# One encoder layer on one core: the first FFN's opening stage fetches its modulation and its first token half ahead, with the operand sums on VectorE

## The chip, the core and the metric

The kernel runs on one core of a Trainium2 chip. The metric is the time of one execution in device microseconds (us), median of several runs; lower is better. The engines go by the names of the profile: PE is TensorE (matmuls; PEld its weight loads), DVE is VectorE, ACT is ScalarE, POOL is GpSimd, SP is SyncE. SP and ACT also issue the DMA transfers of this stage.

## What is computed

One layer of a bidirectional encoder on 1024 tokens of width 1024, in float32: a half-step SwiGLU FFN, a mixer of a convolution group and a differential-attention group, and a second half-step FFN, each with a residual and a LayerNorm behind it. Shift, scale and gate of each sub-layer come from one conditioning vector. The change touches only the beginning of the first FFN:

```python
c_act = jax.nn.silu(c)
mod = (c_act @ w_ada[l] + b_ada[l]).reshape(B, N_SUBLAYERS, 3, D)   # D = 1024, w_ada is 1024 x 9216

def swiglu(h, w_in, w_out):                                         # d_ff = 2816
    gate, up = jnp.split(h @ w_in, 2, axis=-1)
    return (jax.nn.silu(gate) * up) @ w_out

def post_norm_sublayer(x, mod, weight, f, g, b):
    shift, scale, gate = mod[:, 0, None, :], mod[:, 1, None, :], mod[:, 2, None, :]
    y = f(x * (1.0 + scale) + shift)
    return layer_norm(ALPHA * x + weight * (1.0 + gate) * y, g, b)
```

## The kernel before

**Products.** A float32 product is made of three matmuls: each operand is split into a rounded high part (a cast on ACT, `S.copy`) and the rest (a subtraction, on DVE unless told otherwise), and high by high, high by low and low by high are added in PSUM. `split` does this; its two lines show in the profile as L139 and L140. The input product of the FFN runs over 22 tiles `j` of 128 gate and 128 up columns. In each tile the two token halves and the gate/up pair form a 2 x 2 block product, which is done with seven products (A11·B11, A12·B21, S2·T2, S1·T1, S3·T3, S4·B22, A22·T4) over sums and differences of the operands. A product has 4 inner steps of 3 matmuls, each of 128x512; so a tile is 84 such matmuls. Their names in the rows are `fi_<tile>A` and `fi_<tile>S`. The left operands come from the weights (`ra`, `rb` as loaded; `ah`, `al`, `sh`, `sl` as split), the right ones from the modulated tokens and are kept for all 22 tiles: per pair `kk` of 128-row feature blocks (4 pairs) `r_kbh`/`bl` (first token half), `r_kt1h`/`t1l` and `r_kt3h`/`t3l` (differences of the halves) and `r_kb` (the second half's odd block).

**The opening stage.** For each pair `kk`, `first_ada` fetches 2 x 1024 x 256 values of `w_ada` (2 MiB) and `first_x` 1024 tokens x 256 features (1 MiB). `first_mod` makes shift and scale as two columns each, `B0` and `A0`: for some columns DVE adds the eight weighted rows (`ada0a`) and PE sums over partitions with `ones`; for the rest PE multiplies with `c_act` directly. PE transposes the tokens (`hT`), ACT or DVE applies scale and shift (`h`), POOL and DVE form the differences (`right_second`, `right_third`), and the splits follow.

**What sets the order.** Each engine runs its own queue in order; the queues are written by the program and a scheduler. In the opening stage the string `SEQ` gives the order: `a`/`x` fetch a pair, `M13` makes the modulation of pair 1 with 3 of its 4 column blocks on DVE, `H` transposes and modulates both token halves, `R` makes all right operands of the pair with an engine letter for each step, `g` runs four of tile 0's seven products for the pair. So each pair goes through everything before the next. All transfers are issued by SP. Buffers named by `slot` are 30 rotating slots of the tag `h`; the modulation weights of three of the pairs lie in part in the six buffers `sh`/`sl` instead. After the stage, tile 1 is prepared and `in_phase` runs the tiles one after the other: products 1, 2, 6, 5, 7, 3, 4 of tile 0, then those of tile 1, and so on.

Of the kernel before, what the change touches and what calls it, by code (L numbers as in the profile page):

```python
# [44 lines left out]
SEQ = "a0 M03 w0 x0 G0 a1 H0d x1 R0VGVGV M12 x2 a2 H1 M24 S0 g0 a3 R1VGVGG H2 g1 x3 R2VGVGG M33 H3d R3VVVGV g2 g3"  # L46
# [4 lines left out]
def layer_kernel(ctx, tc, a, out):  # L51
# [37 lines left out]
    S.activation(c_act, c_raw, AF.Silu)  # L89
# [190 lines left out]
    def right_first(name, ops, hb, eng=V):  # L280

        hi, lo = slot(f"{name}bh"), slot(f"{name}bl")
        split(hi, lo, hb, eng)
        ops["B11"].append((hi[:, 0], lo[:, 0]))
        ops["B21"].append((hi[:, 1], lo[:, 1]))

# [45 lines left out]
    def in_load(wp, s, w_in, j):  # L332
# [6 lines left out]
        for dst, src in ((ra[:, 0], k1[:, :, g]), (ra[:, 1], k2[:, :, g]), (rb, k1[:, :, u]), (ra[:, 2], k2[:, :, u])):  # L339
            SY.dma_start(dst, src)  # L340
# [353 lines left out]
    with pool("p1a") as wp:  # L694
        in_tags(wp, "ra rb ah al sf sh sl")
        ops = new_ops()
# [3 lines left out]
        def first_ada(kk):  # L700
            raws = []
            for m in range(2):
                for q in range(2):
                    name = f"ada0_{kk}_{m}{q}"
                    if kk == 0 or kk == 3 and m == 1:
                        raw = slot(name, (P, 4, 256), F32)
                    else:
                        raw = wp.tile([P, 4, 256], F32, tag="sl" if q else "sh", bufs=3, name=name)
                    SY.dma_start(raw, w_ada[:, 4 * q : 4 * q + 4, m * D + kk * 256 : m * D + (kk + 1) * 256])
                    raws.append(raw)  # L710
            return raws

        def first_x(kk):
            cols = slice(kk * 256, (kk + 1) * 256)
            xc = []
            for half in range(2):
                x = slot(f"xc{kk}_{half}", (P, 4, 256), F32)
                SY.dma_start(x, x_in[half * H : (half + 1) * H, cols].rearrange("(t p) n -> p t n", p=P))
                xc.append(x)
            return xc  # L720

        def first_mod(kk, raws, n):

            ps = wide(f"ada0p{kk}")
            if n:
                acc = wp.tile([P, 2, 256], F32, tag="ada_acc", bufs=1, name=f"ada0a{kk}")
            parts = [(m, max(0, 4 - n - 2 * m) * P) for m in (0, 1)]
            for j in range(KD):
                for m, lo in parts:
                    if lo >= 256:  # L730
                        continue
                    raw, dst = raws[2 * m + j // 4][:, j % 4, lo:], acc[:, m, lo:]
                    if j == 0:
                        V.tensor_scalar(dst, raw, c_act[:, 0:1], None, ALU.mult)
                    else:
                        V.scalar_tensor_tensor(dst, raw, c_act[:, j : j + 1], dst, ALU.mult, ALU.add)
            for m, lo in parts:
                for e in range(2):
                    es = slice(e * P, (e + 1) * P)
                    o = ps[:, 2 * m + e : 2 * m + e + 1]  # L740
                    if e * P >= lo:
                        PE.matmul(o, lhsT=acc[:, m, es], rhs=ones[:, 0:1], start=True, stop=True)
                        continue
                    for j in range(KD):
                        PE.matmul(
                            o, lhsT=raws[2 * m + j // 4][:, j % 4, es], rhs=c_act[:, j : j + 1],
                            start=j == 0, stop=j == KD - 1,
                        )
# [4 lines left out]
        def first_t(kk, xc, half):  # L753
            ps = wide(f"hT0_{kk}_{half}")
            for e in range(2):
                for i in range(4):
                    o = e * H + i * P
                    PE.transpose(ps[:, o : o + P], xc[half][:, i, e * P : (e + 1) * P], ident)
            return ps

        def first_h(kk, ps, half, HD):
            h = slot(f"h0_{kk}_{half}", dt=F32)
            k = 2 * kk
            h_of(h[:, 0], ps[:, 0:H], A0, B0, k)
            if HD:
                V.tensor_scalar(h[:, 1], ps[:, H:T], A0[:, k + 1 : k + 2], B0[:, k + 1 : k + 2], ALU.mult, ALU.add)
            else:
                h_of(h[:, 1], ps[:, H:T], A0, B0, k + 1)
            return h

        def early(wp, s, w_in, ops):
            order = (("A11", "B11"), ("A12", "B21"), ("S2", "T2"), ("S1", "T1"))
            begun = {}
            ada, xs_, hs, w, L0 = {}, {}, {}, [], {}

            def go(k):
                for left, right in order:
                    if left not in begun:
                        begun[left] = bank(f"fi{s}_0{left}")
                    product(begun[left], L0[left], ops[right], (k,))  # L780

            for tok in SEQ.split():
                c, k, v = tok[0], int(tok[1]), tok[2:]
                if c == "a":
                    ada[k] = first_ada(k)
                elif c == "x":
                    xs_[k] = first_x(k)
                elif c == "w":  # L790
                    w.append(in_load(wp, s, w_in, 0))
                elif c == "G":
                    L0.update(in_gate(wp, s, 0, w[0]))
                elif c == "S":
                    in_sums(wp, s, 0, w[0], L0, G if v else V)
                elif c == "M":
                    first_mod(k, ada[k], int(v))
                elif c == "H":
                    for half in range(2):
                        hs[k, half] = first_h(k, first_t(k, xs_[k], half), half, v == "d")  # L800
                elif c == "R":
                    e = [{"V": V, "G": G}[n] for n in v]
                    right_first(f"r0_{k}", ops, hs[k, 0], e[0])
                    t12 = right_second(f"r0_{k}", ops, hs[k, 0], hs[k, 1], e[1], e[2])
                    last = right_third(f"r0_{k}", ops, hs[k, 0], hs[k, 1], t12, e[3], e[4])
                elif c == "g":
                    go(k)
            raws = in_load(wp, s, w_in, 1)
            with tc.issue_after(last[0]), tc.issue_after(last[1]):
                L1 = in_gate(wp, s, 1, raws)  # L810
                in_sums(wp, s, 1, raws, L1)
            return [L0, L1], (begun, {}), None

# [673 lines left out]
```

## Time and profile before

| | us |
|---|---|
| median of 3 runs (1926.94 to 1928.09) | 1926.99 |
| profiled execution | 1927.3 |
| its span in the trace | 1925.5 |
| outside the span (start and end) | 1.8 |
| PE busy in the span | 1829.6 (95%) |
| DVE busy | 1518.1 (79%) |
| ACT busy | 773.0 (40%) |
| POOL busy | 321.0 (17%) |

The page's row of slices shows PE busy 5 and 8 tenths in the first two of 40 slices (48 us each), and nine tenths or more in nearly all others. An engine's busy time includes matmuls that overlap. The granted clock of PE is 0.974 of full in the mean.

### The profile page before, as it was taken

The numbers are of one execution on the slowest core, as the hardware profiler recorded it, in microseconds if no ns is written. First come the engines' busy times: TensorE is split into PE (matmuls) and PEld (weight loads), VectorE is DVE, ScalarE is ACT, GpSimd is POOL, SyncE is SP. The second block draws the span as 40 slices with busy tenths as digits, with TensorE's granted clock in tenths as the row PEclk, the third lists the DMA queues.
The fourth block names the chain that finished last, engine by engine and source line by source line (L and its number), as shares of the span: only waits on it lengthen the run. The fifth ranks groups of instructions, "written<-read, shape, count | busy, mean of one in ns | idle before, by whom it ended". The sixth has DMA issues, their size and how long they took to land.

```text
span 1925.5 us, 23435 instructions
## 1 busy us (share of the span) xinstructions
PE 1829.6 (95%) x8562; PEld 1512.7 (79%) x8562; DVE 1518.1 (79%) x2306; ACT 773.0 (40%) x1233; POOL 321.0 (17%) x236
## 2 busy tenths in 40 slices
PE   5899999999999999999999877989999999999996
PEld 4688888888888878888788765868887888888885
DVE  8867767765698887999688889898767565569789
ACT  3423333333445442142477761353333333254540
POOL 3200000000000010067376562160000000000000
PEclk7899999999999999999999888989999999999998
DMA  8526545442985332111000033125555333177432
GB/s 252 167 96 212 170 150 175 157 144 89 307 302 155 120 116 66 44 44 34 1 1 1 12 121 99 55 82 168 174 162 175 120 116 120 44 287 275 133 99 83
DMA packets 203699, 246.79 MB, mean 128 GB/s; under 512 B 14122, under 2 KB 124831, under 8 KB 203582
## 3 DMA queue, kind: packets, MB, share of 16 engines
q1 hardware_dynamic: 199082, 231.61, 37.0%
q0 software_dynamic: 2112, 7.34, 1.0%
q10 hardware_dynamic: 2388, 6.33, 0.8%
q8 instruction: 67, 1.10, 0.2%
q14 instruction: 50, 0.41, 0.1%
HBM read 188.08 MB, written 57.15 MB: 127 GB/s over the span
## 4 chain that ended last, share of the span: by engine, by line
PE 70%; DVE 16%; issue 8%; DMA 3%; ACT 2%; POOL 1%; SPq 1%; DVEq 0%; POOLq 0%; ACTq 0%
PE fo L589 19%; PE mo L1294 4%; PE vp L961 2%; DVE mx L1058 2%; PE qp L961 2%; PE fi_16A L378 1%; PE fi_15A L378 1%; PE fi_10A L378 1%; PE fi_6A L378 1%; PE fi_2A L378 1%; PE fi_21A L378 1%; PE fi_19A L378 1%; PE fi_20A L378 1%; PE fi_18A L378 1%; PE fi_17A L378 1%
## 5 line engine op out<-in xcount | busy, mean ns | idle before, releaser
L589 PE MATMUL fo<-wr,gl 128*128 128x512 f32 x1848 | 423.1, 390 | 0.2
L589 PEld LDWEIGHTS fo<-wr,gl 128*128 128x128 f32 x1848 | 345.9, 188 | 75.3 <-DVE pv L632 1.3
L140 DVE TENSOR_TENSOR sl<-sf,sh 128x1024 fp32r<-128x1024 f32 x87 | 109.4, 1259 | 116.0 <-ACT sh L139 115.8
L139 ACT CAST sh<-sf 128x1024 fp32r<-128x1024 f32 x88 | 92.7, 1053 | 207.3 <-issue 31.3
L932 DVE SCALAR_TENSOR_TENSOR cacc<-u,convw,cacc 128x1015 f32<-128x1015 f32 (+14 forms) x120 | 150.7, 1305 | 0.9
L399 POOL DMA_DIRECT2D gd<-gf x8 | 4.5, 567 | 826.6 <-DVE gf L465 826.0
L140 DVE TENSOR_TENSOR gl<-gr,gl 128x512 fp32r<-128x512 f32 x148 | 102.1, 696 | 6.9 <-ACT gl L139 5.5
L139 ACT CAST gl<-gr 128x512 fp32r<-128x512 f32 x148 | 90.5, 617 | 24.3 <-DMA gr<-gd 17.6
L153 DVE SCALAR_TENSOR_TENSOR ada<-adaw,c_act,ada 128x512 f32<-128x512 f32 x98 | 73.2, 747 | 30.9 <-DMA adaw<-in_w_ada_dram 30.0
L1058 DVE TENSOR_REDUCE mx<-sc 128x1 f32<-128x1024 f32 x64 | 76.2, 1215 | 20.4 <-PE sc L1056 20.4
L1060 ACT ACTIVATE p<-sc,mx 128x1024 f32<-128x1024 f32 x64 | 71.4, 1115 | 47.8 <-DVE mx L1058 46.3
L139 ACT CAST ah<-ra 128x1536 fp32r<-128x1536 f32 x44 | 65.0, 1478 | 59.6 <-DMA ra<-in_ffn_w_in_dram 14.9
L140 DVE TENSOR_TENSOR al<-ra,ah 128x1536 fp32r<-128x1536 f32 x44 | 77.0, 1750 | 1.3 <-ACT ah L139 1.2
L427 ACT ACTIVATE gf<-gf 128x512 f32<-128x512 f32 x44 | 27.8, 632 | 124.1 <-DVE gf L426 113.7
L139 ACT CAST wr<-wa 128x512 fp32r<-128x512 f32 x66 | 41.2, 624 | 76.6 <-PE fo L589 76.0
L1294 PE MATMUL mo<-moh,fh 128*128 128x512 f32 x128 | 51.4, 402 | 20.7 <-DVE x L1298 20.1
L140 DVE TENSOR_TENSOR wr<-wa,wr 128x512 fp32r<-128x512 f32 x66 | 45.5, 689 | 27.4 <-ACT wr L139 27.2
L139 ACT CAST wr<-wb 128x512 fp32r<-128x512 f32 x66 | 40.2, 621 | 64.8 <-PE fo L589 51.5
L913 PE MATMUL glu<-hm,gluh 128*128 128x512 f32 x256 | 65.7, 392 | 0.0
L1112 POOL TENSOR_TENSOR p<-p,p 128x1024 f32<-128x1024 f32 x27 | 64.8, 2400 | 1.9
L1129 PE MATMUL av<-vf,aT 128*128 128x128 f32 x512 | 63.4, 278 | 1.2 <-ACT cacc L1190 0.8
L1129 PEld LDWEIGHTS av<-vf,aT 128*128 128x128 f32 x512 | 60.9, 195 | 1.7 <-ACT cacc L1190 1.0
(3505 smaller groups left out, 4775.6 us busy)
## 6 DMA issues: line engine op xcount, KB each, us to landing
gr<-gd SPq DMA_DIRECT2D x148, 256.0 KB, 3.3
ra<-in_ffn_w_in_dram SPq DMA_DIRECT2D x132, 256.0 KB, 3.8
adaw<-in_w_ada_dram SPq DMA_DIRECT2D x56, 512.0 KB, 3.8
gd<-gf SPq DMA_DIRECT2D x102, 256.0 KB, 2.1
rb<-in_ffn_w_in_dram SPq DMA_DIRECT2D x44, 256.0 KB, 3.0
wb<-in_ffn_w_out_dram SPq DMA_DIRECT2D x44, 256.0 KB, 5.4
wa<-in_ffn_w_out_dram SPq DMA_DIRECT2D x44, 256.0 KB, 5.0
gd<-s SPq DMA_DIRECT2D x40, 256.0 KB, 2.0
```

The costliest lines, as they stand in the source:

```text
L139: a = S.copy(hi, x)
L140: b = eng.tensor_tensor(lo, x, hi.bitcast(F32), ALU.subtract)
L153: V.scalar_tensor_tensor(acc, raw[:, jj], c_act[:, n : n + 1], acc, ALU.mult, ALU.add)
L378: pe_last[:] = [PE.matmul(ps, lhsT=w[:, k], rhs=x, start=k == 0 and n == 0 and not more, stop=k == 3 and n == 2, skip_group_check=more,).ins]
L589: PE.matmul(ps, lhsT=g[:, x, ts_], rhs=w[:, y], start=n in (1, 2, 3) and k == i == 0, stop=k == NK - 1 and i == 2, skip_group_check=n not ...
L913: PE.matmul(q[2 * m + h], lhsT=w[:, m * P : (m + 1) * P], rhs=hm[k][h][:, x], start=k == 0 and n == 0, stop=k == KD - 1 and n == 2,)
L932: V.scalar_tensor_tensor(acc[:, lo_t:hi_t], u[:, lo_t + sh : hi_t + sh], convw[:, i, jj : jj + 1], acc[:, lo_t:hi_t], ALU.mult, ALU.add,)
L961: PE.matmul(pss[t], lhsT=hk[:, x, ts_], rhs=w, start=k == 0 and n == 0, stop=k == KD - 1 and n == 2)
L1058: V.tensor_reduce(mx_, ps, axis=AX.X, op=ALU.max, negate=True)
L1060: S.activation(pe, ps, AF.Exp, bias=mx_, accum_out=sm[:, e : e + 1])
L1129: PE.matmul(ps[:, 0:P], lhsT=aT[:, kt], rhs=vf[kt][:, h * P : (h + 1) * P], start=kt == 0, stop=kt == 7)
L1294: pe = PE.matmul(ps, lhsT=x[:, ts_], rhs=w[:, ds_], start=n == 0, stop=n == total - 1)
```

## The change

Four things change, all in the opening stage and in tiles 0 and 1.

- **Fetch.** Every pair's modulation weights go to rotating slots, as four slots of 512 KiB filled by two transfers each. SP first issues, pair by pair, modulation and the first token half (512 tokens), then tile 1's weights, then the second token half of all pairs. Tile 0's weights are issued by ACT behind the first activation.
- **Modulation.** DVE adds six of the eight rows for all four columns of a pair (128x512 each), PE multiplies the last two rows with `c_act` into the same sum.
- **Order.** The first token half of all pairs is done first (`early`): modulation, transpose, scale, split, products A11·B11 and A12·B21 of tile 0. Then `mid` runs A11·B11 and A12·B21 of tile 1, the second token half of the pairs one by one with S2·T2 and S1·T1, and the remaining products of tiles 0 and 1 in turns.
- **Engines.** The differences of the halves, which POOL made for the most part, are on DVE; POOL has no work in the stage. Scale and shift are always on ACT.

```diff
-SEQ = "a0 M03 w0 x0 G0 a1 H0d x1 R0VGVGV M12 x2 a2 H1 M24 S0 g0 a3 R1VGVGG H2 g1 x3 R2VGVGG M33 H3d R3VVVGV g2 g3"
...
-            ps = wide(f"ada0p{kk}")
...
+            ps = bank(f"ada0p{kk}")
+            acc = wp.tile([P, 2, 256], F32, tag="ada_acc", bufs=1, name=f"ada0a{kk}")
+            for j in range(2 * n):
+                raw = raws[j // 2][:, j % 2]
+                if j == 0:
+                    V.tensor_scalar(acc, raw, c_act[:, 0:1], None, ALU.mult)
+                else:
+                    last = V.scalar_tensor_tensor(acc, raw, c_act[:, j : j + 1], acc, ALU.mult, ALU.add)
+            for i in range(4):
+                m, es = i // 2, slice(i % 2 * P, (i % 2 + 1) * P)
+                o = ps[:, i : i + 1]
+                for j in range(2 * n, KD):
+                    PE.matmul(
+                        o, lhsT=raws[j // 2][:, j % 2, m, es], rhs=c_act[:, j : j + 1], start=j == 2 * n, stop=False
+                    )
+                pe = PE.matmul(o, lhsT=acc[:, m, es], rhs=ones[:, 0:1], start=n == 4, stop=True)
...
+            with tc.issue_after(c_silu.ins):
+                raws = [in_load(wp, s, w_in, 0, S)]
+            ada, xb = [], []
+            for kk in range(4):
+                ada.append(first_ada(kk))
+                xb.append(first_x(kk, 0))
+            raws.append(in_load(wp, s, w_in, 1))
+            xc = [first_x(kk, 1) for kk in range(4)]
+            hb, L = [], [{}, {}]
             begun = {}
...
+            for kk in range(4):
+                with tc.issue_after(columns) if kk else nullcontext():
+                    summed, columns = first_mod(kk, ada[kk], 3)
+                    hb.append(first_h(kk, xb[kk], 0))
...
+                copied, rest = right_first(f"r0_{kk}", ops, hb[kk])
+                for left, right in (("A11", "B11"), ("A12", "B21")):
+                    if kk == 0:
...
+        def mid(st):
...
+            for kk in range(4):
+                with tc.issue_after(first["pe"]):
+                    b, h = hb[kk], first_h(kk, first["xc"][kk], 1)
+                t = wp.tile([P, 2, H], F32, tag="t12", bufs=1, name="t12_0") if kk == 0 else slot(f"t12_{kk}", dt=F32)
+                V.tensor_tensor(t[:, 0], h[:, 0], b[:, 0], ALU.subtract)
+                V.tensor_tensor(t[:, 1], h[:, 1], t[:, 0], ALU.subtract)
+                copied, rest = right_t(f"r0_{kk}", ops, 1, t)
...
+            for kk in range(4):
+                b, h, t = hb[kk], hc[kk], t12[kk]
+                right_b22(f"r0_{kk}", ops, h)
+                V.tensor_tensor(h[:, 0], h[:, 1], h[:, 0], ALU.subtract)
+                V.tensor_tensor(h[:, 1], b[:, 1], t[:, 1], ALU.subtract)
+                copied, rest = right_t(f"r0_{kk}", ops, 3, h)
```

The order of instructions shows where the work stands now. **PE, between the modulation of pairs 1 and 2.** `ada0p` are the modulation columns, `fi_0A` tile 0's two products. Before:

```order
L745 MATMUL ada0p_293<-c_act,ada_1_01_238 128x1 x4
L378 MATMUL fi_0A_397<-r_0bh,ah_0_232 128x512
L758 MATMUL hT_1_0_335<-ident,xc_0_268 128x128 x7
L742 MATMUL ada0p_293<-ones,ada0a_294 128x1 x2
L758 MATMUL hT_1_0_335<-ident,xc_0_268 128x128
L378 MATMUL fi_0A_397<-r_0bl,ah_0_232 128x512
```

Now:

```order
L748 MATMUL hT_2_0_390<-ident,xc_0_230 128x128 x8
L380 MATMUL fi_0A_302<-r_1bh,ah_0_294 128x512
L380 MATMUL fi_0A_306<-r_1bh,ah_0_294 128x512
L380 MATMUL fi_0A_302<-r_1bl,ah_0_294 128x512
L380 MATMUL fi_0A_302<-r_1bh,al_0_295 128x512
L380 MATMUL fi_0A_306<-r_1bl,ah_0_294 128x512
L380 MATMUL fi_0A_306<-r_1bh,al_0_295 128x512
L737 MATMUL ada0p_368<-ones,ada0a_369 128x1
L734 MATMUL ada0p_368<-c_act,ada_2_3_227 128x1 x2
```

All six products of a pair, which need that pair's split `r_1bl`, now stand ahead of the next pair's modulation columns; before, a pair's columns were made between them.

**DVE, the same place.** `B` and `A` are shift and scale, `ada0a` the sum over rows. Before:

```order
L140 TENSOR_TENSOR r_0bl<-h_0_0_253,r_0bh 128x1024
L736 SCALAR_TENSOR_TENSOR ada0a_294<-ada_1_11_242,c_act,ada0a_294 128x256 x2
L140 TENSOR_TENSOR r_0t1l<-r_0t_276,r_0t1h 128x1024
L140 TENSOR_TENSOR r_0b_286<-h_0_1_265,r_0b_286 128x512
L750 TENSOR_TENSOR B_105<-ada0p_293,bada 128x2
L751 SCALAR_TENSOR_TENSOR A_104<-ada0p_293,bada 128x2
```

Now:

```order
L739 TENSOR_TENSOR B_106<-ada0p_324,bada 128x2
L740 SCALAR_TENSOR_TENSOR A_105<-ada0p_324,bada 128x2
L727 TENSOR_SCALAR ada0a_369<-ada_2_0_218,c_act 128x512
L729 SCALAR_TENSOR_TENSOR ada0a_369<-ada_2_0_218,c_act,ada0a_369 128x512
L729 SCALAR_TENSOR_TENSOR ada0a_369<-ada_2_1_221,c_act,ada0a_369 128x512 x2
L141 TENSOR_TENSOR r_1bl<-h_1_0_355,r_1bh 128x1024
L729 SCALAR_TENSOR_TENSOR ada0a_369<-ada_2_2_224,c_act,ada0a_369 128x512 x2
L739 TENSOR_TENSOR B_106<-ada0p_368,bada 128x2
L740 SCALAR_TENSOR_TENSOR A_105<-ada0p_368,bada 128x2
```

The splits of the second half are gone from between the pairs, and a pair's row sums start behind the previous pair's `A`.

**DVE, the second token half.** `t_2` are the differences of the halves of pair 2. POOL made them before (these are POOL's rows):

```order
L290 TENSOR_TENSOR r_2t_486<-h_2_1_463,h_2_0_451 128x512
L291 TENSOR_TENSOR r_2t_486<-h_2_1_463,r_2t_486 128x512
L297 TENSOR_TENSOR r_2t_493<-h_2_1_463 128x512
L298 TENSOR_TENSOR r_2t_493<-h_2_0_451,r_2t_486 128x512
L140 TENSOR_TENSOR r_2t3l<-r_2t_493,r_2t3h 128x1024
```

Now, on DVE:

```order
L807 TENSOR_TENSOR t_2_546<-h_2_1_543,h_2_0_399 128x512
L808 TENSOR_TENSOR t_2_546<-h_2_1_543,t_2_546 128x512
L827 TENSOR_TENSOR h_2_1_543<-h_2_1_543 128x512
L141 TENSOR_TENSOR r_2t1l<-t_2_546,r_2t1h 128x1024
L807 TENSOR_TENSOR t_3_565<-h_3_1_562,h_3_0_443 128x512
L808 TENSOR_TENSOR t_3_565<-h_3_1_562,t_3_565 128x512
```

Three of the five moved to DVE beside the first split; the other two (`L828` and the split `r_2t3l`) come in a second round over the pairs, when the first round is done.

## Rows read from the trace of the kernel before

**Rows 1.** Stretches: us, busy PE, PEld, DVE, ACT, POOL (x count), PEclk, DMA, GB/s

```profile
20.00:53.00 33.00, 22.87 (x90) 18.82 (x91) 31.56 (x49) 14.13 (x19) 14.24 (x10) 0.59 0.76 236
...
76.00:103.00 27.00, 27.00 (x119) 22.09 (x118) 25.64 (x36) 10.35 (x13) 0.00 (x0) 1.00 0.56 169
```

**Rows 2.** Chain that ended last, first 140 us: start us, us, what

```profile
33.62 5.81 DVE ada0a L736 x7
...
102.72 5.44 PE fi_2A L378 x24
```

**Rows 3.** SP's waits, first 80 us: total us, times, longest

```profile
SPq L709 <- DVE ada0a L736: 14.9, 2, 7.7
```

**Rows 4.** Stretches of 10 us, columns as in Rows 1

```profile
0.00:10.00 10.00, 4.22 (x19) 4.05 (x19) 4.28 (x14) 1.49 (x2) 0.70 (x6) 1.00 0.82 248
10.00:20.00 10.00, 5.36 (x30) 5.04 (x30) 8.14 (x16) 3.67 (x4) 0.56 (x1) 1.00 1.11 332
20.00:30.00 10.00, 7.35 (x38) 6.47 (x39) 8.74 (x12) 3.85 (x5) 4.67 (x4) 0.57 1.09 348
30.00:40.00 10.00, 5.83 (x21) 4.53 (x19) 9.93 (x17) 6.33 (x8) 5.16 (x4) 0.67 0.47 146
```

**Rows 5.** Instructions on the tile ada, whole span: ns min/median/max

```profile
L153 DVE SCALAR_TENSOR_TENSOR ada<-adaw,c_act,ada x98: 734/746/754, 93.3 to 1540.7; 128x512 f32<-128x512 f32 x98
...
L151 DVE TENSOR_SCALAR ada<-adaw,c_act x14: 471/479/487, 92.3 to 1530.5; 128x512 f32<-128x512 f32 x14
```

**Rows 6.** A group by form, first 103 us: busy us, mean ns

```profile
L736 DVE SCALAR_TENSOR_TENSOR ada0a<-ada,c_act,ada0a 128x256 f32<-128x256 f32 x35 | 23.3, 679 | 0.6
```

**Rows 7.** Timeline, first 60 us: start us, us, engine, instruction

```profile
18.94 4.75 PE L745 MATMUL ada0p<-c_act,ada 128*128 128x1 f32 x32 [0.40 <-DVE h L766]
...
21.25 0.96 DVE L734 TENSOR_SCALAR ada0a<-ada,c_act 128x256 f32<-128x256 f32 x1 [1.05 <-DMA ada<-in_w_ada_dram]
...
30.70 1.22 DVE L140 TENSOR_TENSOR r_0t3l<-r_0t,r_0t3h 128x1024 fp32r<-128x1024 f32 x1
31.11 0.63 PE L378 MATMUL fi_0A<-r_0bl,ah 128*128 128x512 f32 x1
...
31.54 0.63 PE L378 MATMUL fi_0A<-r_0bh,al 128*128 128x512 f32 x1
...
31.96 1.91 PE L758 MATMUL hT<-ident,xc 128*128 128x128 f32 x8
...
33.91 1.45 ACT L277 ACTIVATE h<-hT,B,A 128x512 f32<-128x512 f32 x2 [1.85 <-PE hT L758]
...
36.18 1.05 ACT L139 CAST r_1bh<-h 128x1024 fp32r<-128x1024 f32 x1
...
56.23 2.27 DVE L140 TENSOR_TENSOR r_2bl<-h,r_2bh 128x1024 fp32r<-128x1024 f32 x1
```

**Rows 8.** Timeline, 60 to 86 us, columns as in Rows 7

```profile
65.61 1.09 PE L378 MATMUL fi_0A<-r_3bh,ah 128*128 128x512 f32 x2 [3.42 <-ACT r_3bh L139]
...
75.14 1.75 DVE L140 TENSOR_TENSOR al<-ra,ah 128x1536 fp32r<-128x1536 f32 x1
...
77.41 0.68 DVE L357 TENSOR_TENSOR sf<-ra,rb 128x512 f32<-128x512 f32 x1
...
78.01 0.68 DVE L356 TENSOR_TENSOR sf<-sf,ra 128x512 f32<-128x512 f32 x1
...
81.28 0.39 PE L378 MATMUL fi_1A<-r_1bh,ah 128*128 128x512 f32 x1
...
81.51 0.39 PE L378 MATMUL fi_1A<-r_1bl,ah 128*128 128x512 f32 x1
```

**Rows 9.** Stretches of 1 us, PE alone: busy (x count), PEclk, DMA, GB/s

```profile
52.00:53.00 1.00, 1.00 (x5) 0.93 1.07 291
...
57.00:58.00 1.00, 0.27 (x3) 1.00 1.14 317
...
66.00:67.00 1.00, 0.71 (x2) 0.50 0.00 0
```

More of the change, by code (lines that the diff above doesn't have):

```diff
@@ L2 @@
+from contextlib import nullcontext
 import concourse.bass as bass
@@ L282, in right_first @@
         hi, lo = slot(f"{name}bh"), slot(f"{name}bl")
-        split(hi, lo, hb, eng)
+        last = split(hi, lo, hb, eng)
         ops["B11"].append((hi[:, 0], lo[:, 0]))
         ops["B21"].append((hi[:, 1], lo[:, 1]))
+        return last
     def right_second(name, ops, hb, hc, eng=G, lo=V):
@@ L330, in layer_kernel, with in_load @@
     raw_pool = {}
-    def in_load(wp, s, w_in, j):
+    def in_load(wp, s, w_in, j, q=SY):
         rp = raw_pool.get(s, wp)
@@ L695, in layer_kernel @@
         in_tags(wp, "ra rb ah al sf sh sl")
+        wp.tile([P, 2, H], F32, tag="t12", bufs=1, name="t12_")
         ops = new_ops()
@@ L701, in first_ada @@
             raws = []
[L702 to L710, printed above, removed]
@@ L711, in first_ada @@
-            return raws
[L713 to L720, printed above, removed]
-        def first_mod(kk, raws, n):
-            ps = wide(f"ada0p{kk}")
[L725 to L748, printed above, removed]
@@ new lines, in first_ada, with first_x @@
+            for q in range(4):
+                raw = slot(f"ada0_{kk}_{q}", (P, 2, 2, 256), F32)
+                for m in range(2):
+                    src = w_ada[:, 2 * q : 2 * q + 2, m * D + kk * 256 : m * D + (kk + 1) * 256]
+                    SY.dma_start(raw[:, :, m], src)
+                raws.append(raw)
+            return raws
+        def first_x(kk, half):
+            x = slot(f"xc{kk}_{half}", (P, 4, 256), F32)
+            src = x_in[half * H : (half + 1) * H, kk * 256 : (kk + 1) * 256]
+            SY.dma_start(x, src.rearrange("(t p) n -> p t n", p=P))
+            return x
@@ L751, in first_mod, with first_h @@
             V.scalar_tensor_tensor(A0[:, ks], ps[:, 2:4], 1.0, bcol(0, 1)[:, ks], ALU.add, ALU.add)
-        def first_t(kk, xc, half):
+            return last.ins, pe.ins
+        def first_h(kk, x, half):
             ps = wide(f"hT0_{kk}_{half}")
@@ L757, in first_t @@
                     o = e * H + i * P
-                    PE.transpose(ps[:, o : o + P], xc[half][:, i, e * P : (e + 1) * P], ident)
-            return ps
-        def first_h(kk, ps, half, HD):
+                    PE.transpose(ps[:, o : o + P], x[:, i, e * P : (e + 1) * P], ident)
             h = slot(f"h0_{kk}_{half}", dt=F32)
[L763 to L768, printed above, removed]
+            for e in range(2):
+                h_of(h[:, e], ps[:, e * H : (e + 1) * H], A0, B0, 2 * kk + e)
@@ L769, in first_h @@
             return h
+        first = {}
         def early(wp, s, w_in, ops):
-            order = (("A11", "B11"), ("A12", "B21"), ("S2", "T2"), ("S1", "T1"))
-            begun = {}
[L774 to L778, printed above, removed]
-                        begun[left] = bank(f"fi{s}_0{left}")
[L780 to L812, printed above, removed]
+            with tc.issue_after(c_silu.ins):
[5 more added lines that the diff above has]
+            raws.append(in_load(wp, s, w_in, 1))
@@ new lines, in early @@
+            xc = [first_x(kk, 1) for kk in range(4)]
+            hb, L = [], [{}, {}]
+            begun = {}
+            for kk in range(4):
[3 more added lines that the diff above has]
+                if kk == 0:
+                    with tc.issue_after(summed):
+                        L[0].update(in_gate(wp, s, 0, raws[0]))
+                copied, rest = right_first(f"r0_{kk}", ops, hb[kk])
+                for left, right in (("A11", "B11"), ("A12", "B21")):
+                    if kk == 0:
+                        begun[left] = bank(f"fi{s}_0{left}")
+                    product(begun[left], L[0][left], ops[right], (kk,))
+                if kk == 0:
+                    with tc.issue_after(summed):
+                        in_sums(wp, s, 0, raws[0], L[0])
```

44 lines of the change are left out of this document (42 added, 2 removed).

## The prediction

> **What bounds the kernel now.** I read the slices of the page first, which put the loss into the first 100 us, then the busy time of stretches there, then the chain of waits, the timeline of each engine, and SP's waits. From 76 us on PE works without a pause at its upper level, 27.0 of 27.0 us [rows 1], and the chain from there is PE alone; tile 1's last product ends and tile 2 begins at 102.7 us [rows 2]. From 20 to 53 us PE works 22.9 of 33 us at a mean granted clock of 0.59, while DVE works 31.6 [rows 1]: there DVE is the bound. Two things load it. The row sums of the modulation stand in the chain [rows 2], and they are slow where POOL works beside them: 35 of them took 0.679 us in the mean [rows 6], and a split that takes 1.22 us alone took 2.27 us beside a POOL operation [rows 7]. And the fetch stops: SP waited 14.9 us in two places until DVE had read modulation weights out of a buffer [rows 3], so that the transfers fell from 348 GB/s to 146 [rows 4]. Behind tile 1 PE's queue holds the same rows in both kernels, so the question is one number: at what time does tile 1 end in the changed kernel, against 102.7.
>
> **What the change removes and adds.** The profiled execution took 1927.3 us, 0.3 over the median of 1927.0; I make the sum against it and take the 0.3 off at the end. Less than 0.2% (3.9 us) can't be told from no change.
>
> *Fetch.* Modulation and first token half of a pair are 2.62 MB. Up to 20 us 5.8 MB have passed (248 and 332 GB/s over 10 us each), then 348 GB/s [rows 4]. In the new order pair 1's third slot is complete when 5.28 MB have passed (pair 0's 2.62, tile 0's weights 1.05, three quarters of pair 1's 2.10), and pairs 2 and 3 follow every 7.5 us. In before, the wait for such a slot (0.5 MB later in the row, 5.77 MB, passed at 19.9 us) ended at 21.25 [rows 7], so a transfer counts 1.35 us after its last byte. That gives 19.9, 27.4 and 34.9 us for the third slots of pairs 1 to 3, and 41 to 47 us for tile 1's weights and the second half. All of it has slots of its own, so SP waits only for older transfers.
>
> *DVE's load.* It takes over 14 half operations of 0.60 us (the step between two starts) [rows 8] and two splits of 1.14 from POOL, 10.7 us. It gives up the mixed row sums (23.3 us for their largest group) [rows 6] for 4 x (0.48 + 5 x 0.75) = 16.9 us [rows 5], and the slowing beside POOL goes. So DVE has some ten us less to do. That is no gain by itself, because of the next part.
>
> *The chain through a pair.* By the order, a pair's modulation columns stand behind the six products of the pair before on PE, and these wait for the split `bl` on DVE, which stands behind four of the next pair's row sums; those wait for the previous `A`. So each pair goes round: four row sums 0.51 + 3 x 0.78 = 2.85 (0.03 between dependent ones is an estimate), split 1.22, four products at 0.43 (the step from 31.11 to 31.54) 1.7, ten column products at 0.15 (32 in 4.75) 1.65 [rows 7] with the end, `B` and `A` 0.23, three hand-overs at 0.05: 7.7 us. The transposes, 1.6 of eight, and scale, shift and cast on ACT (1.45 + 1.05) [rows 7] lie beside the row sums. Fetch, at 7.5 us, lies inside as well.
>
> *Start.* Tile 0's weights share the bandwidth with pair 0, so its last slot counts at 13.6 and the first `A` stands at 15.2. Then DVE has tile 0's sums, `al`, two splits, pair 1's row sums and `r_0bl`: 4 x 0.60 + 1.67 + 2 x 1.14 + 0.48 + 3.9 + 1.22, with hand-overs 11.3, until 26.5 [rows 5, 7, 8]. Four products and twelve column products: pair 1's `A` at 30.5, pair 2's at 38.2, pair 3's at 45.9. Scale, cast, split and four products behind it, 5.8: tile 0's first two products end at 51.7. If the loop ran at fetch pace it would be 43.
>
> *Second half, first round.* PE goes through tile 1's A11·B11 with the first eight transposes: at 0.43 and 0.2 apiece [rows 7] until its level rises, and then at the upper one, until 57.4. [...] Then ACT scales, 1.45, DVE subtracts, ACT casts 1.05, DVE splits 1.22: `r_0t1l` at 62.3. A pair's round is two subtractions 1.3, cast 1.05, split 1.14 and hand-overs, 3.6 us; with one evacuation of tile 1 among them (0.6) the fourth split ends at 73.6. PE has six products per round, 1.4 us at 0.227 each [rows 8].
>
> *Second round.* Tile 1's sum, cast and split come first, 5.6 until the first `t3l` at 79.2; then 3.5 per pair (small split 0.6, subtraction 0.7, cast 1.05, split 1.14) and 0.7 once, where ACT waits for tile 1's products: 90.6. PE, with 47 products (10.7 us) in these 17 us, waits for it.
>
> *Tail.* Three more DVE operations, 1.9, until S3's bank is read: 92.4. Tile 0's A22 12 products, 2.7; its end frees the buffer for tile 2's cast (1.5, an estimate by width from 1.05 for two thirds of it), `al` 1.75, sum 0.60, split 1.14 and a read of the bank 0.68, until 101.0, while PE makes tile 1's S3 and S4 by 100.6. A22 of tile 1 is 2.7: 103.7, less one product of tile 2 already done, 103.5.
>
> **Sum.** 103.5 - 102.7 = 0.8 us later: 1927.3 + 0.8 - 0.3 = 1928 us. What the fetch and the lighter DVE give the three chains give back. Unknown sizes: the lower level of PE may end earlier or later. If PE were at the upper level from 33 us, the loop is 7.0 instead of 7.7 and the end 99.2; the hand-overs at 0.10 instead of 0.05 add about 2.
>
> **PE's clock, row and rule.** The granted clock rose to 2.4 GHz at 52 us and stayed there through 57 to 58 us, where PE worked 0.27 of 1 us; at 66 to 67 it stood at 0.50, which is 1.2 GHz [rows 9], after PE had been idle for 3.4 us up to 65.6 [rows 8]. So the short pauses were borne and the long one was not. The rounds of the second half leave PE 2.2 us idle of 3.6, in between. The sum above keeps the clock up from 56 us. The Trainium skill ("TensorE: Matmul & The Clock Gate", section "HAM oscillation — how this bites in real kernels") describes a loop in which each burst of matmuls is shorter than the wait behind it, and every burst then starts at the lower clock. By the row tile 1 ends at 103.5 us, 1928; by the rule at 110.7, 1935, which is the first rival below.
>
> **Rivals.**
> 1. *The clock falls in the second half (slower).* It falls at about 72, and as PE only works in short runs until 92, it comes back at 97. Tile 1's 20 products behind the first sum take 8.6 instead of 4.6 us and hold up ACT, which stands behind them; the tail's first products run at 0.43: the end is 110.7, 1935 us. If it comes back at 82, the end is 106.4, 1931. It decides from where the fall lasts into the tail. For it: PE's share of 40% in the rounds; against: 57 to 58 us. Chance 0.28.
> 2. *The pairs run at fetch pace (faster).* Should the loop be shorter than 7.5 us and the second half start when its operands are there, tile 0's first products end at 43 and all behind moves 9 us ahead: 94.5, 1919. For it: DVE has ten us less work and POOL's slowing is gone; against: the order, which lets no pair's columns pass the products of the pair before. Chance 0.13.
> 3. *PE reaches its upper level in the loop (a little faster).* In each round PE works 5.2 us without a pause (four products, ten columns, two columns, eight transposes), and before the change it rose at 52 us in a full stretch [rows 9]; against it are the pauses of a us between. End 99.2, 1923.5; on the edge of what can be told. Chance 0.14.
> 4. *The fetch is not ahead after all.* The ACT queue's transfers delay pair 0, or a slot isn't free. Of 1 us later fetch nothing comes out in the loop, whose pairs wait for products; so it lies within the first forecast.
>
> **How the numbers follow.** The forecast, 1925 to 1931 by itself, has 0.45; 1 has 0.28, 2 and 3 have 0.27 together. Faster by over 0.2%: all of 2 and some half of 3, 0.19. Slower: rival 1 nearly whole, 0.27. The rest, 0.54, is no change. The range leaves out rival 2's full size and rival 1's longest: 1922.5 to 1934.5.
>
> **What the new profile should show.** Third slots of pairs 1 to 3 landed by 20, 27.5 and 35 us and SP's waits for DVE gone; no DVE split above 1.3 us; `A` of pairs 1 to 3 some 7.7 us apart, with DVE waiting for PE ahead of each; the four splits `t1l` 3.6 us apart, `t3l` 3.5; tile 2's first full stretch from about 103.5. The prediction is wrong if `A` comes every 7.5 us or less, or if tile 1's products behind 76 us show 0.43 between starts.

## The result, and the profile after

The changed kernel took 1938.28 us in the median of 4 runs (1936.89 to 1939.75); the kernel before, on the same chip, 1926.97 (4 runs, 1922.49 to 1928.09). The ratio is 1.0069, its 95% interval 1.0057 to 1.0081: slower by 0.6 to 0.8%, where 1928 was predicted. The profiled execution of the changed kernel took 1936.89 us, its span is 1935.1.

Stretches of the changed kernel, columns as in [rows 1]; the first four answer to [rows 4], the last two to [rows 1]:

```profile
0.00:10.00 10.00, 0.35 (x1) 0.18 (x1) 2.89 (x5) 1.49 (x2) 0.70 (x6) 1.00 0.80 238
10.00:20.00 10.00, 7.11 (x32) 6.74 (x32) 4.92 (x11) 2.52 (x2) 0.00 (x0) 1.00 1.11 339
20.00:30.00 10.00, 3.98 (x13) 3.07 (x14) 8.65 (x11) 3.44 (x4) 0.00 (x0) 1.00 1.10 348
30.00:40.00 10.00, 9.71 (x41) 8.39 (x39) 4.03 (x8) 2.49 (x3) 0.00 (x0) 1.00 1.12 331
...
20.00:53.00 33.00, 26.32 (x99) 22.20 (x99) 19.50 (x29) 8.42 (x10) 0.00 (x0) 1.00 1.03 308
76.00:103.00 27.00, 20.53 (x62) 12.75 (x61) 19.30 (x25) 13.80 (x19) 0.00 (x0) 0.81 0.04 11
```

The fetch does what the change is for: 331 GB/s from 30 to 40 us in place of 146. VectorE is busy for 19.5 us of the 33 from 20 to 53 in place of 31.6. And TensorE, which was the engine with pauses, now works 9.71 of 10 us from 30 to 40: the bound has moved to it. From 76 to 103 us, where it had no pause before, it now waits for 6.5 us.

The chain of waits that ended last shows where tile 1 ends:

```profile
104.64 4.35 PE fi_0A L380 x12
108.99 2.74 PE fi_1A L380 x12
111.73 2.72 PE fi_1S L380 x12
114.68 2.82 PE fi_1A L380 x12
117.50 5.21 PE fi_2A L380 x23
```

Tile 2 runs on from 117.5 us, with one product made already, so tile 1 ends at 117.3, against 102.7 in [rows 2] and the 103.5 of the forecast. For the experiments I use a later mark that all kernels share, the start of tile 3's first product, 14.6 us later than before. Before, and now:

```profile
121.60 0.39 PE L378 MATMUL fi_3A<-r_0bh,ah 128*128 128x512 f32 x1
136.19 0.39 PE L380 MATMUL fi_3A<-r_0bh,ah 128*128 128x512 f32 x1
```

The measured difference is 11.3 us of the medians and 13.3 by the ratio, most of these 14.6. The two traces differ by only 9.6 us in their spans, since the rest behind the mark took 1803.9 us before and 1798.9 now. In the twelve other traces it took 1799.0 to 1802.7, so I read these 5 us as the spread between executions and not as time that the change gives back; no run shows which it is.

The timeline of one turn of the first half's loop, with the first pair's last products ahead of it (start, length, engine, line, out <- in, in brackets the idle time before and what ended it):

```profile
28.85 0.79 PE L380 MATMUL fi_0A<-r_0bl,ah 128*128 128x512 f32 x1 [2.44 <-DVE r_0bl L141]
...
30.72 0.85 PE L734 MATMUL ada0p<-c_act,ada 128*128 128x1 f32 x4
...
35.87 0.16 DVE L739 TENSOR_TENSOR B<-ada0p,bada 128x2 f32<-128x2 f32 x1 [7.08 <-PE ada0p L737]
35.94 0.15 DVE L740 SCALAR_TENSOR_TENSOR A<-ada0p,bada 128x2 f32<-128x2 f32 x1
...
38.76 1.22 DVE L141 TENSOR_TENSOR r_1bl<-h,r_1bh 128x1024 fp32r<-128x1024 f32 x1
...
40.04 0.79 PE L380 MATMUL fi_0A<-r_1bl,ah 128*128 128x512 f32 x1
...
41.91 0.42 PE L737 MATMUL ada0p<-ones,ada0a 128*128 128x1 f32 x2
...
42.19 0.99 PE L734 MATMUL ada0p<-c_act,ada 128*128 128x1 f32 x4
...
43.47 0.99 PE L734 MATMUL ada0p<-c_act,ada 128*128 128x1 f32 x4
...
46.21 0.16 DVE L739 TENSOR_TENSOR B<-ada0p,bada 128x2 f32<-128x2 f32 x1 [4.78 <-PE ada0p L737]
...
56.55 0.16 DVE L739 TENSOR_TENSOR B<-ada0p,bada 128x2 f32<-128x2 f32 x1 [4.78 <-PE ada0p L737]
```

`B` comes at 35.87, 46.21 and 56.55: a turn takes 10.34 us, not 7.7, and ahead of each `B` VectorE waits for TensorE's column products (L734, L737), 4.78 us of 10.34. The column products are the thing to look at. For each of four column blocks the program issues two products of L734 and one of L737, and the trace shows them as four and two records: **a float32 product with one column is two records.** The first block's two products of L734 stand ahead of the transposes, the other ten behind the six products of the pair before. A block starts 1.28 us after the one before (42.19 to 43.47), so a product takes 0.43 us, and a pair's twelve take 5.1.

### The profile page after: what moved, and what is told of

It reads as the page before. It is cut to its first block, busy times and chain, and to the rows that moved or that the text cites. A ratio compares the mean times of both kernels' runs of the same rounds, so it can differ in the third digit from the quotient of the medians.

```text
span 1935.1 us, 23424 instructions
## 1 busy us (share of the span) xinstructions
PE 1834.1 (95%) x8570; PEld 1515.0 (78%) x8570; DVE 1510.7 (78%) x2283; ACT 776.6 (40%) x1238; POOL 287.7 (15%) x220
## 4 chain that ended last, share of the span: by engine, by line
PE 72%; DVE 15%; issue 7%; DMA 2%; ACT 2%; POOL 1%; SPq 0%; DVEq 0%; POOLq 0%; ACTq 0%
PE fo L591 19%; PE mo L1321 4%; PE vp L988 2%; DVE mx L1085 2%; PE qp L988 2%; PE fi_15A L380 1%; PE fi_13A L380 1%; PE fi_12A L380 1%; PE fi_6A L380 1%; PE fi_10A L380 1%; PE fi_2A L380 1%; PE fi_21A L380 1%; PE fi_19A L380 1%; PE fi_20A L380 1%; PE fi_18A L380 1%
## 5 line engine op out<-in xcount | busy, mean ns | idle before, releaser
L140 ACT CAST wr<-wb 128x512 fp32r<-128x512 f32 x66 | 40.2, 621 | 64.4 <-PE fo L591 51.0
```

What stands on the lines that cost most here:

```text
L140: a = S.copy(hi, x)
```

## Experiments

**Theory:** the twelve column products stand on the path of every pair at 0.43 us each. **Rivals:** VectorE, which took over sums and differences, is late; TensorE's clock is low; the fetch, with the first tile's weights on another queue, holds pairs back; the order, not the products, costs. The table has for each kernel the start of the last pair's `A`, of tile 3's first product, the median and the ratio to the kernel before on the same chip (whose medians were 1923.9 to 1927.0).

| kernel | last `A` | tile 3 | us | ratio (95%) |
|---|---|---|---|---|
| before | | 121.60 | 1926.97 | |
| changed kernel | 56.63 | 136.19 | 1938.28 | 1.0069 (1.0057-1.0081) |
| 1 eight sums | 51.14 | 129.74 | 1932.95 | 1.0048 (1.0036-1.0061) |
| 2 four sums | 64.41 | 144.91 | 1944.66 | 1.0102 (1.0086-1.0117) |
| 3 differences on GpSimd | 57.18 | 141.91 | 1941.28 | 1.0087 (1.0073-1.0101) |
| 4 weights on SyncE | 55.49 | 135.92 | 1938.03 | 1.0070 (1.0057-1.0082) |
| 5 sums ahead | 45.43 | 128.90 | 1931.31 | 1.0036 (1.0023-1.0048) |
| 6 the same, six sums | 46.69 | 129.23 | 1929.90 | 1.0028 (1.0017-1.0040) |
| 7 spare products | 56.84 | 132.92 | 1935.03 | 1.0053 (1.0040-1.0066) |
| 8 sums ahead, spare | 44.64 | 123.02 | 1927.01 | 1.0013 (1.0004-1.0022) |
| 9 VectorE's order | 44.28 | 125.12 | 1929.03 | 1.0023 (1.0014-1.0032) |
| 10 the same, spare | 43.40 | 119.42 | 1922.67 | 0.9993 (0.9984-1.0002) |
| 11 second half early | 43.69 | 119.12 | 1922.33 | 0.9988 (0.9979-0.9997) |
| 12 before, spare | | 120.96 | 1922.00 | 0.9991 (0.9982-1.0000) |

**1 and 2: fewer and more column products.**

```diff
-                    summed, columns = first_mod(kk, ada[kk], 3)
+                    summed, columns = first_mod(kk, ada[kk], 4)    # 1; in 2: 2
```

> Edit: all eight rows of a pair are summed on VectorE, TensorE keeps four column products for each pair (one per column block) in place of twelve. Column theory (the twelve column products at 0.43 us each stand on the path of every pair): a loop loses eight of them, 3.4 us, and gains two row sums, 1.5 us, so 10.3 us becomes about 8.8, A of the last pair comes at about 52 instead of 56.6, tile 2 starts 4 to 5 us earlier, and the total is 3 to 6 us below the changed kernel (1932 to 1935). VectorE theory (the sums and differences that VectorE took over set the pace): each pair costs 1.5 us more, A of the last pair at about 61, total 4 to 6 us above the changed kernel (1942 to 1944). If neither holds and the clock alone sets it: no change beyond 1 us.

> Edit: four of a pair's eight rows are summed on VectorE, TensorE gets twenty column products for each pair in place of twelve. Column theory: eight more products of 0.43 us in each loop, 10.3 us becomes about 13.8, A of the last pair at 67 to 70 instead of 56.6, total 10 to 13 us above the changed kernel (1948 to 1951). VectorE theory: 1.5 us less for each pair, A of the last pair at about 52, total 4 to 6 us below the changed kernel. Clock theory alone: within 2 us, unless the extra products raise the clock.

Timeline of the run with eight sums:

```profile
33.62 0.16 DVE L739 TENSOR_TENSOR B<-ada0p,bada 128x2 f32<-128x2 f32 x1 [3.67 <-PE ada0p L737]
...
40.81 1.05 PE L737 MATMUL ada0p<-ones,ada0a 128*128 128x1 f32 x8 [0.95 <-DVE ada0a L729]
...
41.90 0.16 DVE L739 TENSOR_TENSOR B<-ada0p,bada 128x2 f32<-128x2 f32 x1 [1.15 <-PE ada0p L737]
```

Timeline of the run with four sums:

```profile
34.08 1.84 PE L734 MATMUL ada0p<-c_act,ada 128*128 128x1 f32 x8
35.78 0.57 PE L737 MATMUL ada0p<-ones,ada0a 128*128 128x1 f32 x2
36.21 1.84 PE L734 MATMUL ada0p<-c_act,ada 128*128 128x1 f32 x8
...
54.13 0.78 PE L380 MATMUL fi_0A<-r_1bl,ah 128*128 128x512 f32 x1
```

With four column products a turn is 8.3 and 9.2 us, tile 3 comes 6.5 us earlier (4 to 5 were expected for tile 2), and part of the wait changes sides: TensorE now waits 0.95 us for VectorE's sums. The four products of this turn also ran at TensorE's upper level, in 1.05 us. With twenty, a block of five takes 2.13 us (34.08 to 36.21), again 0.43 a product, and tile 3 comes 8.7 us later. VectorE has more work in the first and less in the second; its theory has both signs wrong. The column theory has both signs right, and the first run within a us at the last `A`. The second run missed its sizes: `A` came at 64.4, ahead of the 67 to 70 expected, and the total is 1944.7 us in place of 1948 to 1951, since the turns grew by 0.6 and 2.4 us and not by 3.4. The trace shows a reason that the edit doesn't name: a pair's last four products (`r_1bl`, 54.13) now stand behind the next pair's column products, so the order moved too.

**3 and 4: two other parts undone.** In 3 the four differences of a pair in the second half go back to GpSimd; in 4 the first tile's weights go back to SyncE's queue, behind the first pair.

```diff
-                V.tensor_tensor(t[:, 0], h[:, 0], b[:, 0], ALU.subtract)
+                G.tensor_tensor(t[:, 0], h[:, 0], b[:, 0], ALU.subtract)
...
-            with tc.issue_after(c_silu.ins):
-                raws = [in_load(wp, s, w_in, 0, S)]
...
+                if kk == 0:
+                    raws.append(in_load(wp, s, w_in, 0))
```

> Edit: the four differences of a pair in the second half go back to GpSimd, everything else as in the changed kernel. Column theory: the first half is untouched (A of the last pair at 56.6); in the second half GpSimd's operations are longer than VectorE's 0.68 us, so a round grows from 3.7 to 4 to 5 us and the total is 0 to 5 us above the changed kernel (1938 to 1943). VectorE theory: the rounds get shorter by about 1 us each, tile 2 starts 3 to 6 us earlier, total 1932 to 1935.

> Edit: the first tile's weights are fetched on SyncE's queue behind the first pair, as in the kernel before, in place of ScalarE's queue; everything else as in the changed kernel. Column theory: the last pair's data land about 3 us later than now but still more than 10 us ahead of their use, so A of the last pair stays at 56 to 58 and the total within 2 us of the changed kernel. Fetch theory (the pace of the fetches sets the first half): later pairs come 3 us later, total 2 to 4 us above the changed kernel, or, if the fetch of the first pair gains, A of the first pair comes 1 to 2 us earlier and the total is as much lower.

Timeline of the run with the differences on GpSimd:

```profile
73.93 1.63 POOL L807 TENSOR_TENSOR t<-h,h 128x512 f32<-128x512 f32 x1 [0.60 <-ACT h L278]
75.64 1.27 POOL L808 TENSOR_TENSOR t<-h,t 128x512 f32<-128x512 f32 x1
...
78.02 1.23 DVE L141 TENSOR_TENSOR r_1t1l<-t,r_1t1h 128x1024 fp32r<-128x1024 f32 x1 [3.59 <-ACT r_1t1h L140]
```

GpSimd's subtraction takes 1.27 to 1.63 us and VectorE waits 3.59 us for what follows from it: tile 3 comes 5.7 us later. This part of the change is good. The queue makes the first `A` 1.9 us earlier (15.65 in place of 17.56) and next to nothing at the end (135.92): the pace of the fetch isn't what costs in the changed kernel. How far such marks vary by themselves is seen in the first `A` of runs 3 and 7, whose edits lie behind it: 18.10 and 18.27.

**5 and 6: the order, with few and with many column products.** The next pair's sums go to a second buffer ahead of the splits, a pair's six products stand behind the next pair's column products, and the first tile's operand sums come after the last split. 5 has eight sums on VectorE, 6 has six, as the changed kernel.

```diff
+                if kk < 3:
+                    with tc.issue_after(done):
+                        acc, _ = first_sums(kk + 1, ada[kk + 1], 4)    # in 6: 3
...
+                else:
+                    with tc.issue_after(done), tc.issue_after(columns):
+                        products(kk - 1)
...
+                in_sums(wp, s, 0, raws[0], L[0])
```

> Edit: eight row sums on VectorE as in the run with eight sums; besides, the sums of the next pair go to a second buffer and ahead of the splits, TensorE's six products of a pair stand behind the next pair's column products, and the first tile's operand sums come after the last pair's split. Column theory with order: no column product and no product of a pair is left on the path from one A to the next, so the pace is that of the fetch (7.3 us a pair) or of VectorE (seven to eight us a pair): A of the four pairs at about 17, 26, 33 and 41, tile 2 at 98 to 103, total 1920 to 1926. If the fetch or ACT's chain holds it back instead: A of the last pair stays near 50 and the total near 1932.

> Edit: the same order as the run with the sums ahead, but with six row sums on VectorE and twelve column products for each pair on TensorE, as in the changed kernel. Column theory: TensorE at its lower level has 1.95 us of transposes, 2.6 us of products and 5.15 us of column products for each pair, 9.7 us, and so sets the pace: A of the last pair at about 50 to 55, total 7 to 10 us above the run with eight sums in this order (1929 to 1934). Order theory (the place of the sums and products is what costs, not the column products): within 2 us of that run.

Timeline of the run with six sums:

```profile
33.37 0.77 PE L741 MATMUL ada0p<-c_act,ada 128*128 128x1 f32 x4
34.01 0.36 PE L744 MATMUL ada0p<-ones,ada0a 128*128 128x1 f32 x2
34.23 0.58 PE L741 MATMUL ada0p<-c_act,ada 128*128 128x1 f32 x4
...
34.90 0.58 PE L741 MATMUL ada0p<-c_act,ada 128*128 128x1 f32 x4
...
38.37 0.66 PE L755 MATMUL hT<-ident,xc 128*128 128x128 f32 x2 [1.54 <-DMA xc<-in_x_dram]
...
42.66 0.63 PE L380 MATMUL fi_0A<-r_1bl,ah 128*128 128x512 f32 x1
...
44.29 0.28 PE L744 MATMUL ada0p<-ones,ada0a 128*128 128x1 f32 x2
```

Here my sum failed: 6 isn't 7 to 10 us behind 5 but level with it. (Its total fell into the 1929 to 1934 expected only because 5 was slower than expected; that is luck.) So the number of column products is not what costs by itself. In two of three turns they ran at TensorE's upper level: a block of three takes 0.67 us (34.23 to 34.90), 0.22 a product, half of the 0.43. And in the second turn only two wide products stand ahead of them. In the third turn the order did not do what I expected of it: the last four products of the first pair and all six of the second (`r_1bl`, 42.66) stand ahead of the last pair's column products (44.29), and all of this waited until 38.4 us for the tokens (38.6 in 5), so the fetch is part of the path there.

Both kernels fell short of the expectation of 5. Its last `A` came at 45.4 us in place of 41, tile 3 at 128.9, and the total is 1931.3 in place of 1920 to 1926; besides the third turn, VectorE then made the first tile's operand sums, which had only been put off.

Runs 1, 5 and 6 with the changed kernel make a square. Fewer column products in the old order bring tile 3 forward by 6.5 us (1), the new order with all twelve by 7.0 (6), both together by 7.3 (5). At the last `A` it is 5.5, 9.9 and 11.2 us. So either step takes most of the same wait away, and the second adds little to the first.

**7 and 12: the clock.** In 7 six products of 512 columns that nobody reads go into each of the eight rounds of the second half. 12 is a control: the kernel before with twenty such products.

```diff
+        def spare(ps, x=None):
+            w, x = first["L"][0]["A11"][0], x or first["ops"]["B11"][0][0]
+            for n in range(6):
+                PE.matmul(ps[:, 0:H], lhsT=w[:, n % 4], rhs=x, start=True, stop=True)
```

> Edit: the changed kernel, and in each of the eight rounds of the second half six spare products of 512 columns into a bank that nobody reads, so that TensorE is busier in its waits. Clock theory: the granted clock doesn't fall at 80 and 104 us, the products there run at 0.23 us in place of 0.43, tile 2 starts 3 to 4 us earlier (113 to 114 in place of 117.3), total 1934 to 1936. If the clock isn't what costs there, or the spare products stand in the way: tile 2 at 117 to 121, total 1938 to 1942. The first half is untouched: A of the last pair at 56 to 58.

> Edit: the kernel before, with twenty spare products of 512 columns into a bank that nobody reads, in TensorE's waits at 62 to 72 us (twelve behind the third pair's last product, four behind the last pair's first six and four ahead of its last four). Clock reading: the granted clock doesn't fall at 66 us, the products there run at 0.23 us in place of 0.43, tile 3 starts 1 to 3 us before 121.6, total 1 to 3 us below the kernel before. If VectorE alone sets the pace there: within 1 us. If the spare products stand in the way: 1 to 3 us above.

Timeline of the changed kernel in the second half:

```profile
78.69 0.40 PE L380 MATMUL fi_0S<-r_2t1h,sh 128*128 128x512 f32 x1
...
80.18 0.60 PE L380 MATMUL fi_0S<-r_2t1l,sh 128*128 128x512 f32 x1
...
92.55 0.59 ACT L436 COPY u<-fi_1A 128x512 f32<-128x512 f32 x1 [4.10 <-PE fi_1A L380]
94.11 1.23 DVE L141 TENSOR_TENSOR r_1t3l<-h,r_1t3h 128x1024 fp32r<-128x1024 f32 x1 [3.40 <-ACT r_1t3h L140]
...
105.24 0.63 PE L380 MATMUL fi_0A<-r_0t3l,ah 128*128 128x512 f32 x1
105.66 0.63 PE L380 MATMUL fi_0A<-r_0t3h,al 128*128 128x512 f32 x1
```

Stretches of 5 us of the changed kernel, columns as in [rows 1]:

```profile
75.00:80.00 5.00, 2.33 (x8) 1.32 (x9) 4.39 (x7) 3.33 (x5) 0.00 (x0) 1.00 0.00 0
80.00:85.00 5.00, 4.09 (x10) 2.10 (x8) 4.39 (x7) 1.96 (x3) 0.00 (x0) 0.52 0.00 0
...
100.00:105.00 5.00, 2.04 (x6) 0.86 (x6) 4.53 (x7) 2.56 (x3) 0.00 (x0) 0.91 0.55 134
105.00:110.00 5.00, 5.00 (x18) 3.94 (x18) 3.49 (x6) 1.26 (x2) 0.00 (x0) 0.75 0.95 285
```

The same stretches of the run with spare products (7):

```profile
75.00:80.00 5.00, 5.00 (x25) 3.74 (x24) 4.38 (x6) 4.01 (x6) 0.00 (x0) 1.00 0.00 0
80.00:85.00 5.00, 4.72 (x19) 2.98 (x18) 4.38 (x7) 2.09 (x4) 0.00 (x0) 1.00 0.00 0
...
100.00:105.00 5.00, 5.00 (x23) 4.13 (x23) 5.00 (x8) 1.38 (x2) 0.00 (x0) 1.00 0.89 268
```

In the changed kernel TensorE works 2.33 of 5 us up to 80, then the granted clock is 0.52 and products start 0.43 us apart; it falls once more ahead of tile 0's last twelve products, which take 4.35 us in place of 2.7. With the spare products it stays at 1.00 from 65 us on, and tile 3 comes 3.3 us earlier, as expected. So the clock in the second half costs about 3 us, and the rest is elsewhere. The Trainium skill ("TensorE: Matmul & The Clock Gate", section "HAM oscillation — how this bites in real kernels") describes a loop in which each burst of matmuls is shorter than the wait behind it and starts at the lower clock. The trace agrees in part: in the eight rounds the clock fell twice, at 80.2 and 104.1 us, and was back at 90.4 and 107.5; it did not fall at every burst. In the control the first twelve of the twenty came only at 64.5 us and the clock fell for 3 us all the same. Its gain, 0.6 us at tile 3 (1 to 3 expected), is at the edge of what the runs can tell. Its total is 1.9 us below the kernel before, inside the expected range, but not for the reason expected, since the clock did fall.

**8 to 11: the parts together.** 8 is 5 with the spare products. 9 is 5 with VectorE's order written out (the first tile's differences in the wait for the first column products, splits behind the next pair's sums); 10 is 9 with the spare products; 11 also puts the second half's first transposes directly behind the first half's last. The edit of 9 moves TensorE's work as well: the products of pairs 1 to 3 stand behind all column products, and a pair's transposes behind its own.

```diff
+                if kk < 3:
+                    with tc.issue_after(summed), tc.issue_after(rests[0] if kk == 2 else summed):
+                        acc, summed = first_sums(kk + 1, ada[kk + 1], 4)
...
+                ahead = first_t(0, xc[0], 1)    # 11
```

> Edit: the run with the sums ahead, and the same spare products in the second half. Column and clock theory together: 2 to 4 us below the run with the sums ahead, 1917 to 1923, so below the kernel before. If the spare products stand in the way: 0 to 3 us above the run with the sums ahead.

> Edit: the run with the sums ahead, and VectorE's order written out: the first tile's operand differences stand in the wait for the first pair's column products, the first pair's split follows the third pair's sums, the second tile's gate split follows the last pair's split, and TensorE takes a pair's column products ahead of its transposes. Reading so far (VectorE's own work is what is left of the first half once the column products are off the path): A of the last pair at 41 to 44 in place of 45.4, the second half's rounds begin about 5 us earlier, tile 3 at 122 to 126 in place of 128.9, total 1925 to 1929. If VectorE's order isn't what holds it: tile 3 at 128 to 130, total 1930 to 1932.

> Edit: the run before it, with the spare products of the second half. Column, clock and VectorE's order together: tile 3 at 117 to 121 in place of 123.0 with the spare products alone, total 1921 to 1925, so level with the kernel before or up to 3 us below it. If VectorE's order isn't what holds it: 1926 to 1928.

> Edit: the run with VectorE's order and the spare products, and the transposes of the second half's first pair stand on TensorE directly behind those of the first half's last pair. Reading so far (after the last split VectorE waits 3 us for the second half's first modulation, which waits for TensorE's order): the first difference of the second half at 48 to 51 in place of 54.8, tile 3 at 114 to 118 in place of 119.4, total 1917 to 1921, below the kernel before by more than 0.2%. If the transposes then wait for the fetch and hold the products up: tile 3 at 119 to 121, total 1922 to 1925.

At tile 3 the remedies add up: 7.3 us for the order with eight sums (5), 5.9 more for the clock (8 against 5, where the clock alone gave 3.3 in 7), and 3.6 to 3.8 for the order of 9 (10 against 8, 9 against 5), in which VectorE's and TensorE's part can't be told apart. 8 missed its expectation, 1927.0 us for 1917 to 1923, as 5 had; 9 (1929.0) came to the upper edge of its range and 10 (1922.7) into it. 11 moved the first difference to 51.0 us, where 48 to 51 was expected, but the second pair's modulation then waited for its transposes, which stand behind twelve products of tile 1 and six spare ones (1.5 us), and tile 3 gained 0.3 us of the 1 to 5 expected. The total, 1922.3, missed the 1917 to 1921. Timeline of 11:

```profile
51.04 0.68 DVE L853 TENSOR_TENSOR t<-h,h 128x512 f32<-128x512 f32 x1
...
56.21 1.45 ACT L278 ACTIVATE h<-hT,B,A 128x512 f32<-128x512 f32 x2 [1.65 <-PE hT L755]
57.02 0.69 DVE L853 TENSOR_TENSOR t<-h,h 128x512 f32<-128x512 f32 x1 [1.75 <-ACT h L278]
```

Run 11 is 0.12% below the kernel before (0.03 to 0.21), too little to call it faster by the bound of the prediction, and 12 shows that spare products alone give the kernel before about as much.

## Why the prediction was wrong

- **The step that failed** is the term "ten column products at 0.15 (32 in 4.75) 1.65" in the chain through a pair. The 32 of [rows 7] are records, and they are 16 products. They also ran partly at the upper level, while I put the six products beside them at the lower one; in the kernel before, in stretches of 1 us as in [rows 9]:

```profile
20.00:21.00 1.00, 1.00 (x11) 1.00 1.10 350
...
22.00:23.00 1.00, 1.00 (x6) 0.50 1.10 349
```

  Measured in the changed kernel: 0.43 each, ten in 4.3 us. That is 2.65 us more per turn, and the turn is 2.64 longer than forecast (10.34 for 7.7). The same price stands in the twelve between `r_0bl` and the next `A` (5.1 us for 1.8) and in the first pair's twelve, which began at 12.1 us, earlier than the 13.6 assumed, and still put the first `A` at 17.6 for 15.2. The last pair's `A` is 10.7 us late (56.6 for 45.9), of the 13.8 by which tile 1 ends later than forecast. The mechanism, a chain in which no pair's columns pass the products before them, was right: run 1 shows what the columns cost in it, run 6 that it gives way when the order does.
- **The clock** was rival 1 and in part came true beside it. It fell at 80.2 us and was back at 90.4. Tile 1's products stood 0.43 us apart there (from 87.5 to 89.7), which the prediction had named as a sign of being wrong; they held ACT for 4.10 us, and VectorE waited 3.40 us for `r_1t3h`, as that rival says. The clock fell again ahead of A22 of tile 0, 4.35 us for 2.7. Run 7 prices it at 3.3 us. So the rival's 7.2 us was too much and the forecast's 0 too little. The sum has TensorE at its upper level from 56 us, and no run shows that time; by its steps it rose at about 63.2, and tile 1's first products with their transposes then took 4.2 us in place of 5.7.
- **Rival 2**, the pairs at fetch pace, was far off: 10.34 us a pair against 7.5. **Rival 3**, the upper level in the loop, did not come true in the changed kernel, and did in two turns of run 6, where it made a block of column products half as long.
- **Right:** the fetch (above; SyncE's waits for VectorE are gone, its longest wait now is 2.7 us for a transfer), splits at 1.22 to 1.23 us with GpSimd idle, VectorE waiting for TensorE ahead of each `A`, rounds of the second half at 3.74, 4.33 and 3.73 us between `t1l` splits (70.26, 74.00, 78.33, 82.06) against 3.6 and once 4.2.
- **Slips that cost nothing:** the terms of the start add up to 11.95 us, not 11.3; the trace took 11.2 (17.56 to 28.79) because one of the first tile's sums ran ahead of the first `A`, so the 11.3 was luck. The terms of the loop add up to 7.8, not 7.7. "Some ten us less" for VectorE doesn't follow from the rows given with it; over the whole span it is 7.4 (1510.7 us busy for 1518.1).
- **The unknown sizes** were bounded from the wrong side: the range held a faster loop and longer hand-overs, but no higher price for the column products, for which the trace of before had the row.

Open is how much of a turn is the level and how much the order. In run 6, and in one turn of run 1, TensorE reached its upper level as well, and no run raises the level in the first half in the changed kernel's order. At 0.22 a product, ten would take 2.2 us in place of 4.3; that is an estimate from run 6.

## What to carry to other kernels

Count instructions in the program before dividing a group's time by its records, and price an operation at the engine's level in the place where it will stand. Where work is moved from a loaded engine to one that had pauses, add up the receiving engine's whole turn first: here, at the lower level, transposes 1.95, six products 2.6 and twelve column products 5.1 make 9.7 of TensorE's 10.34 us, and that sum alone, against a fetch of 7.5, would have shown the new bound. It holds only for the level that it is made at: the same sum failed for run 6. One-column products that end a reduction are best put ahead of the wide work that doesn't need them (run 6, 7.0 us), or on the engine that makes the sums (run 1, 6.5 us).

## What the runs showed of the hardware

- The granted clock stands at 1.00 in the record of the changed kernel from 0 to 80 us, but products start 0.43 us apart until 63, the same step as at 82 to 85 where the record says 0.50. In run 7, with the same first half, the record says 0.50 from 32 to 64 us. Ahead of the first change in the record the level has to be read from the steps.
- TensorE was busy 9.71 of 10 us from 30 to 40 us and stayed at the lower level; one-column products made up 5.1 us of a turn of 10.34. In run 6, with the same products in another order, it reached the upper level at about 33 us. In the kernel before, the granted clock fell at 21.4 us, within a row of 16 one-column products that ran without a pause (18.94 to 23.69).
- A float32 product with one column costs as much as one with 512 columns of the split operands: 0.43 us at the lower level. At the upper level both take half, 0.22 (run 6) and 0.23 us.
